# Memory's keys and values from split operands, and a later change of PSUM pools, in a Conformer and RWKV-7 streaming block

## The chip, the cores and the metric

The kernel runs on one core of one Trainium2 chip. The metric is the device time of one execution in microseconds (us), as the median of three runs. The engines are TensorE (PE, with its weight loads as PEld), VectorE (DVE), ScalarE (ACT), GpSimd (POOL) and SyncE (SP, which issues nearly all DMAs). [...]

## The reference, cut to what matters

One layer of a streaming encoder: x is 1024 frames by 1024 features, the memory 256 tokens by 1024.

```python
h = rmsnorm(x, g_mix)
p = h @ w_in                                  # 1024 conv columns, 1696 RWKV columns
u = p[:, :512] * sigmoid(p[:, 512:1024])      # conv branch
u = depthwise_causal_conv(u, conv_w, 31 taps) + conv_b
y_conv = silu(layernorm(u) * ln_g + ln_b)
y_rwkv = rwkv7(p[:, 1024:])                   # a recurrence over 1024 steps, 8 heads of 64
x = x + concat(y_conv, y_rwkv) @ w_out
k, v = rmsnorm(mem) @ wk, rmsnorm(mem) @ wv   # 4 heads of 256
x = x + softmax_attention(rmsnorm(x) @ wq, k, v) @ wo
x = x + relu(rmsnorm(x) @ w_ff1) ** 2 @ w_ff2
return rmsnorm(x, g_final)
```

## The kernel before

The kernel is one long program of a tile framework. The source emits instructions with a priority, which by default counts up in the order of the source. A planner then puts every engine's instructions in one fixed order: it plays the program through, and whenever an engine is free it hands it the ready instruction of the lowest priority number. On the chip each engine runs its list in that order and waits by semaphores only for real data. `at` and `shifted` (L421, L411) emit a piece under another priority. `fill` (L789) emits "side" steps 200 earlier than where they stand, and `tap` (L611) emits one step of the convolution 1000 earlier.

A float32 product is done in two ways. Most go through `mm3` (L75): both operands are split beforehand into a high part, rounded to the format `float32r` by ACT, and the rest, by a subtraction, and three products (high by high, high by low, low by high) add up in PSUM. A few take float32 as it is.

The stages and the buffers that order them:

- `mixer_in` (L525) computes `w_in`'s products for the first 512 frames and the convolution's for all. `tap_steps` (L615) is the convolution: five pieces (one channel block of 128 in two halves, three whole), each one multiplication (L646) and 30 multiply-adds on DVE (L649), of which 29 have PSUM (`sum`, two banks) as accumulator. At its end `mixer_in` calls `tap(1)` 31 times.
- Then the first PSUM pool `ps0` (banks `mm` 2, `pr` 2, `ep` 1, `cp` 1, `sum` 2) is closed and the second one, `ps` (`mm` 2, `pr` 2, `ep`, `cp`, `py`, `us` 1 each), is opened.
- The recurrence goes over eight tiles of 128 frames. `front(e)` (L772) is a tile's preparation (`rwkv_prepare`, L801: norms at L825 to L838, the products L871) and the triangular solve on DVE (`rwkv_solve`, L888: transposes L896, sixteen pairs L916 and L917, L921, L928, products L932 and L937, and the copy L938, which ends it). `chain(e)` (L778) is the recurrence proper, two chunks of 64 frames. Tile buffers `AR` and `BK` are two deep, so `front(e + 2)` waits for `chain(e)`.
- The order written out by hand: front 0, front 1, chain 0, front 2, chain 1, front 3, chain 2, and so on. Between them `fill` takes steps of a side generator, by the table `F`. The first side generator, `second_half` (L601), has twelve steps: each is one product of `w_in` for the second 512 frames, 24 matmuls of 128x512 (L81 to L83), with its weight split by ACT (L266) and POOL (L267), and a mixing step on ACT and DVE (L516, L517). `F` gives four of these steps to front 0, three to front 1 and the other five to chain 0.
- The second side generator (`side`, L341, from front 4 on in the source) interleaves `memory_side` (L449) with `conv_norms` (L712), then does `w_out` (`mix_steps`, L1051). `memory_side` takes float32 as it is: 8 + 8 weight blocks (`wkv`) of 128 columns against the normed memory (L461), and for each head the value times `wo` (L491, L494), which goes to DRAM as `dv`. `conv_norms` does the layer norm of the convolution for the eight tiles, on the buffers `x1`.
- Attention, the MLP (a seven-product scheme) and the last norm follow.

Of the kernel before, what the change touches and what calls it, by code (L numbers as in the profile page):

```python
# [17 lines left out]
P = 128  # L18
S = 1024
D = 1024  # L20
# [31 lines left out]
class Trunk:  # L52
# [220 lines left out]
    def run(self):  # L273
# [13 lines left out]
        with ctx:  # L287
# [32 lines left out]
            first.__exit__(None, None, None)  # L320
            self.ps = ctx.enter_context(self.pool("ps", space=PSUM, reuse_waits="tile"))
# [16 lines left out]
            x1 = {i: px1.tile([P, D], F32, name=f"x1_{i}") for i in (0, 4, 1, 5, 2, 6, 3, 7)}  # L338
            at = []

            def side():  # L341
                pn = push(right, "pN")
                norms = self.conv_norms(pn, x1)
                self.skip(pn, 288)
                pw, w = push(right, "pW0"), [None, None]
                for k, _ in enumerate(self.memory_side(push(right, "pM"), pw, w)):
                    if k % 2:
                        next(norms, None)
                    yield
                for _ in norms:  # L350
# [98 lines left out]
    def memory_side(self, pM, pw, wo):  # L449
        nc, a, ps = self.nc, self.a, self.ps  # L450

        mem = self.memT

        def m4(shape, name):
            return pM.tile(shape, F32, tag="m4", name=name, bufs=5)

        def half(name, c, dst):
            w = m4([P, KC, P], "wkv")
            nc.sync.dma_start(w, self.cols(name, c * P, P))
            for k in range(KC):  # L460
                nc.tensor.matmul(dst, w[:, k, :], mem[k // 4][:, k % 4, :], start=k == 0, stop=k == KC - 1)  # L461

        def features(name, g, out):
            pp = self.bank(ps, "mm")
            half(name, 2 * g, pp[:, 0:M])
            yield
            half(name, 2 * g + 1, pp[:, M:])
            nc.scalar.copy(out, pp.rearrange("p (e m) -> p e m", m=M))
            yield

        for g in range(4):
            t = pM.tile([P, 2, M], F32, tag="kv", name="kT", bufs=2)
            yield from features("wk", g, t)
            nc.sync.dma_start(self.dk[2 * g : 2 * g + 2].rearrange("e p m -> p e m"), t)
        for h in range(4):
            vT = pM.tile([P, 2, M], F32, tag="kv", name="vT", bufs=2)
            yield from features("wv", h, vT)
            if h == 2:
                wo[0] = self.out_weights(pw, lambda: m4([P, D], "wst")[:, 0:512], 0, 0)
            w = []  # L480
            for i in range(2):
                t = m4([P, D], "wo")
                nc.sync.dma_start(t, a["wo"][0, (2 * h + i) * P : (2 * h + i + 1) * P, :])
                w.append(t)
            for m in range(2):
                vs = m4([P, D], "vs")
                for n in range(2):
                    pp = self.bank(ps, "mm")
                    cs = slice(n * 512, n * 512 + 512)
                    for i in range(2):  # L490
# [34 lines left out]
    def mixer_in(self, pc, pb, px, pl, pW, pz, hT):  # L525
# [72 lines left out]
        for _ in range(31):  # L598
            self.tap(1)
# [999 lines left out]
```

## Time and profile before

| what | value |
|---|---|
| three runs | 1552.95, 1553.52, 1554.87 us; median 1553.52 |
| the profiled execution | 1554.8 us |
| its span, first to last instruction | 1553.1 us |
| mean granted TensorE clock | 0.982 |
| TensorE matmul | busy 1482.1 us (95%) |
| VectorE, ScalarE, GpSimd | busy 1119.4, 674.0, 519.4 us |

The profiled execution took 1554.8 us, of which 1.7 us lie outside its span. Matmuls are pipelined: the duration of a record is longer than the time until the next can start, so the number of matmuls in a stretch says more of PE's load than its busy time. A matmul on plain float32 leaves two records.

### The profile page before, as it was taken

The page shows a single profiled execution, that of the slowest core. Times are in us where ns is not written, and L with a number is a line of the kernel's source. Part 1 is how long each engine was busy: PE and PEld are TensorE (multiplying, and loading weights), DVE is VectorE, ACT ScalarE, POOL GpSimd, SP SyncE. Part 2 cuts the span into 40 slices and gives each one's busy share as a digit, 9 for nine tenths or more (in the row PEclk, how much of TensorE's full clock was granted, in tenths as well). Part 3 has the DMA queues.
Part 4 walks back from the last instruction along what each step waited for, and adds up shares of the span by engine and source line. Part 5 has one row for each costly group of instructions (what it writes and reads, how often), then busy time and mean ns, then how long its engine had stood idle before and what let it go on. Part 6 is the DMA issues. An engine that isn't in the chain of part 4 may idle for free. (4 is left out here: it accounts for less than half of the span.)

```text
span 1553.1 us, 22049 instructions
## 1 busy us (share of the span) xinstructions
PE 1482.1 (95%) x8114; PEld 1211.6 (78%) x8114; DVE 1119.4 (72%) x1701; ACT 674.0 (43%) x1243; POOL 519.4 (33%) x436
## 2 busy tenths in 40 slices
PE   5999995999999999999999979999999899999998
PEld 4777883778777778878888858888888788888886
DVE  5989995778788897464543797666666488587995
ACT  5433332423465543344222345555555445444454
POOL 4112453423335342331110064544444330003372
PEclk9999997999999999999999979999999999999999
DMA  7155563464234422221110223544444496552323
GB/s 211 55 169 173 153 175 102 134 190 123 62 116 143 143 96 76 88 89 48 35 42 27 81 96 116 172 157 153 150 153 152 170 366 204 184 183 87 103 81 122
DMA packets 175725, 201.14 MB, mean 130 GB/s; under 512 B 12191, under 2 KB 116951, under 8 KB 175618
## 3 DMA queue, kind: packets, MB, share of 16 engines
q1 hardware_dynamic: 168706, 187.15, 38.4%
q10 hardware_dynamic: 6912, 12.59, 2.2%
q8 instruction: 64, 1.05, 0.3%
q14 instruction: 43, 0.35, 0.1%
HBM read 139.92 MB, written 59.77 MB: 129 GB/s over the span
## 5 line engine op out<-in xcount | busy, mean ns | idle before, releaser
L649 DVE SCALAR_TENSOR_TENSOR sum<-u,cw,sum 128x1024 f32<-128x1024 f32 (+1 forms) x145 | 155.7, 1074 | 4.1
L1261 POOL TENSOR_TENSOR p<-p,p 128x512 f32<-128x512 f32 x32 | 61.0, 1935 | 196.6 <-DVE p L1520 171.8
L267 POOL TENSOR_TENSOR wlo<-wst,whi 128x1024 fp32r<-128x1024 f32 (+2 forms) x34 | 80.9, 2383 | 126.9 <-ACT whi L266 99.8
L73 DVE TENSOR_TENSOR s<-f,s 128x512 fp32r<-128x512 f32 x48 | 50.9, 1063 | 53.1 <-ACT s L72 53.1
L1366 ACT ACTIVATE y<-y 128x512 f32<-128x512 f32 x64 | 40.4, 632 | 80.8 <-DVE y L1261 73.3
L266 ACT CAST whi<-wst 128x1024 fp32r<-128x1024 f32 (+2 forms) x34 | 35.0, 1030 | 84.9 <-PE mm L82 25.9
L81 PE MATMUL mm<-hT1hi,whi 128*128 128x512 f32 (+1 forms) x128 | 51.5, 402 | 19.8 <-DVE z L517 19.8
L916 DVE TENSOR_TENSOR fs<-xt,PL 128x4 f32<-128x4 f32 (+15 forms) x128 | 61.8, 483 | 8.1 <-ACT PL L908 5.4
L461 PE MATMUL mm<-memT,wkv 128*128 128x256 f32 x256 | 63.4, 397 | 2.2 <-DMA wkv<-in_wk_dram 2.2
L95 POOL TENSOR_TENSOR rsr<-rsv,mhalf 128x1 f32<-128x1 f32 x26 | 15.2, 585 | 145.2 <-DVE rsv L90 135.6
L1261 POOL TENSOR_TENSOR s<-y 128x512 f32<-128x512 f32 x32 | 41.2, 1308 | 59.8 <-ACT y L1367 56.4
L72 ACT CAST s<-y 128x512 fp32r<-128x512 f32 x57 | 35.2, 621 | 58.3 <-PE us L83 26.8
L73 DVE TENSOR_TENSOR s<-y,s 128x512 fp32r<-128x512 f32 x57 | 44.9, 789 | 21.5 <-ACT s L72 21.5
L72 ACT CAST r<-y 128x512 fp32r<-128x512 f32 x55 | 33.8, 620 | 53.4 <-PE cp L83 23.2
L461 PEld LDWEIGHTS mm<-memT,wkv 128*128 128x128 f32 x256 | 48.4, 197 | 10.1 <-DMA wkv<-in_wk_dram 2.5
L72 ACT CAST s<-w 128x512 fp32r<-128x512 f32 x69 | 42.5, 618 | 22.9 <-DMA w<-in_w_ff_dram 8.0
L73 DVE TENSOR_TENSOR r<-y,r 128x512 fp32r<-128x512 f32 x55 | 42.6, 779 | 13.1 <-ACT r L72 13.0
L83 PE MATMUL mm<-hT1hi,wlo 128*128 128x512 f32 (+1 forms) x128 | 51.4, 401 | 0.0
L82 PE MATMUL mm<-hT1lo,whi 128*128 128x512 f32 (+1 forms) x128 | 50.9, 398 | 0.0
L72 ACT CAST s<-f 128x512 fp32r<-128x512 f32 x64 | 37.9, 620 | 27.6 <-DVE f L1261 22.1
L1104 POOL TENSOR_TENSOR wql<-wst,wqh 128x1024 fp32r<-128x1024 f32 x8 | 20.4, 2546 | 82.9 <-ACT wqh L1103 82.9
L917 DVE TENSOR_REDUCE xt<-fs 128x2 f32<-128x4 f32 (+15 forms) x128 | 45.2, 353 | 3.2
(1102 smaller groups left out, 4921.1 us busy)
## 6 DMA issues: line engine op xcount, KB each, us to landing
y<-da SPq DMA_DIRECT2D x112, 256.0 KB
wst<-in_w_in_dram SPq DMA_DIRECT2D x32, 512.0 KB
w<-in_w_ff_dram SPq DMA_DIRECT2D x56, 256.0 KB
da<-y ACTq DMA_DIRECT2D x48, 256.0 KB
ms<-in_w_ff_dram SPq DMA_DIRECT2D x16, 512.0 KB
w<-in_w_ff_dram SPq DMA_DIRECT2D x16, 512.0 KB
da<-s SPq DMA_DIRECT2D x32, 256.0 KB
da<-y SPq DMA_DIRECT2D x32, 256.0 KB
```

The lines of the kernel that those rows point to most:

```text
L72: nc.scalar.copy(hi, src)
L73: (eng or nc.vector).tensor_tensor(lo, src, f32(hi), ALU.subtract)
L81: nc.tensor.matmul(ps, lh, rh, start=first and k == 0, stop=False)
L82: nc.tensor.matmul(ps, lh, rl, start=False, stop=False)
L83: nc.tensor.matmul(ps, ll, rh, start=False, stop=last and k == n - 1)
L267: nc.gpsimd.tensor_tensor(lo, st, f32(hi), ALU.subtract)
L461: nc.tensor.matmul(dst, w[:, k, :], mem[k // 4][:, k % 4, :], start=k == 0, stop=k == KC - 1)
L649: nc.vector.scalar_tensor_tensor(acc if t < TAPS - 1 else out, u[:, t : t + w], self.cw[:, t * 4 + c : t * 4 + c + 1], acc, ALU.mult, ALU.add,
L916: nc.vector.tensor_tensor(tmp, x, rows, ALU.mult)
L917: nc.vector.tensor_reduce(xt[:, 0:m, 2 * k : 2 * k + 2], tmp, AX.X, ALU.add)
L1261: (eng or self.nc.vector).tensor_tensor(out, x, y, op)
L1366: nc.scalar.activation(c, c, AF.Relu)
```

## The change

The change has two parts. First, the pool `ps0` stays open over front 0 and front 1: the 31 calls of `tap` at the end of `mixer_in` go, the taps not yet emitted come with the side steps of these two fronts, and `ps` is opened ahead of chain 0. Second, `memory_side` splits the memory, its weights and the values and uses `mm3`; its weights' parts live in four tiles of its own and in the four `x1` buffers of tiles 4 to 7. So the convolution's norms get only four steps within it, and the other twelve after it; the split of `w_out`'s first block moves from the third head to the end.

```diff
@@ run
-            first.__exit__(None, None, None)
-            self.ps = ctx.enter_context(self.pool("ps", space=PSUM, reuse_waits="tile"))
             self.ring = None
...
             self.front(0)
             self.front(1)
+            for _ in self.taps:
+                pass
+            first.__exit__(None, None, None)
+            self.ps = ctx.enter_context(self.pool("ps", space=PSUM, reuse_waits="tile"))
             for e in range(3):
...
-            for _ in self.taps:
-                pass
             pop(right, 4)
...
-                for k, _ in enumerate(self.memory_side(push(right, "pM"), pw, w)):
-                    if k % 2:
-                        next(norms, None)
+                for k, _ in enumerate(self.memory_side(push(right, "pM"), pw, w, [(px1, f"x1_{i}") for i in range(4, 8)])):
+                    if 26 <= k < 30:
+                        next(norms)
                     yield
+                for i in range(4, 8):
+                    x1[i] = px1.tile([P, D], F32, tag=f"x1_{i}", name=f"x1_{i}")
                 for _ in norms:
                     yield
@@ memory_side
+        rooms = itertools.cycle([(pM, f"w{i}") for i in range(4)] + list(spare))
...
+        def parts(src, view):
+            st, hi, lo = stage(), room(), room()
+            nc.sync.dma_start(view(st), src)
+            nc.scalar.copy(hi, st)
+            nc.gpsimd.tensor_tensor(lo, st, f32(hi), ALU.subtract)
+            return view(hi), view(lo)
...
-                nc.tensor.matmul(dst, w[:, k, :], mem[k // 4][:, k % 4, :], start=k == 0, stop=k == KC - 1)
+                self.mm3(pp[:, e * M : (e + 1) * M], [(wh[:, k, :], wl[:, k, :]) for k in range(KC)], mem)
...
+            vh, vl = (pw.tile([P, 2, M], F32R, tag=t, name="vT") for t in ("wh3", "wl3"))
+            self.split(vh, vl, pp)
+            w = [parts(a["wo"][0, (2 * h + i) * P : (2 * h + i + 1) * P, :], lambda z: z) for i in range(2)]
...
-                    for i in range(2):
-                        nc.tensor.matmul(
-                            pp, vT[:, i, m * P : (m + 1) * P], w[i][:, cs], start=i == 0, stop=i == 1
-                        )
-                    nc.scalar.copy(vs[:, cs], pp)
+                    self.mm3(pp, [(vh[:, i, ms], vl[:, i, ms]) for i in range(2)], [tuple(z[:, cs] for z in w[i]) for i in range(2)])
+                    vs = pw.tile([P, HALF], F32, tag=("wh2", "wl2")[n], name="vs")
+                    nc.scalar.copy(vs, pp)
+                    nc.sync.dma_start(self.dv[h, m][:, cs], vs)
                     yield
-                nc.sync.dma_start(self.dv[h, m], vs)
+        wo[0] = self.out_weights(pw, lambda: stage(HALF), 0, 0)
@@ mixer_in
-        for _ in range(31):
-            self.tap(1)
```

The memory itself is split once: two ACT copies of 128x1024 to a room, four DVE subtractions of 128x512, and two more ACT copies of 128x1024 of the high part.

## Rows read from the trace of the kernel before

**Rows 1.** The page, busy time: engine, us (share) xinstructions

```profile
PE 1482.1 (95%) x8114; PEld 1211.6 (78%) x8114; DVE 1119.4 (72%) x1701; ACT 674.0 (43%) x1243; POOL 519.4 (33%) x436
```

**Rows 2.** By stretch: length, busy (x) of PE PEld DVE ACT POOL, PEclk, DMA, GB/s

```profile
232.50:252.20 19.70, 0.00 (x0) 0.00 (x0) 19.21 (x17) 3.85 (x6) 4.65 (x2) 0.56 0.10 31
252.20:318.00 65.80, 65.72 (x317) 50.67 (x317) 38.29 (x60) 21.83 (x37) 32.11 (x22) 0.97 0.47 135
...
339.80:552.20 212.40, 206.94 (x1777) 165.12 (x1779) 174.95 (x365) 108.31 (x211) 81.69 (x99) 0.98 0.42 124
552.20:659.00 106.80, 106.00 (x876) 88.23 (x877) 74.24 (x133) 39.00 (x79) 38.26 (x34) 1.00 0.27 86
...
1000.00:1200.00 200.00, 200.00 (x884) 165.65 (x883) 124.54 (x158) 104.08 (x171) 95.14 (x75) 1.00 0.46 153
```

**Rows 3.** Timeline of DVE, 211 to 253 us: start, us, instruction xcount [idle before]

```profile
211.87 0.74 DVE L517 SCALAR_TENSOR_TENSOR z<-mm,pcol,z 128x511 f32<-128x511 f32 x1
212.53 3.93 DVE L649 SCALAR_TENSOR_TENSOR sum<-u,cw,sum 128x1024 f32<-128x1024 f32 x3
...
229.09 21.16 DVE L649 SCALAR_TENSOR_TENSOR sum<-u,cw,sum 128x1024 f32<-128x1024 f32 x16
...
251.48 1.40 DVE L517 SCALAR_TENSOR_TENSOR z<-mm,pcol,z 128x511 f32<-128x511 f32 x2
```

**Rows 4.** Timeline of PE, 220 to 253 us

```profile
220.68 0.39 PE L81 MATMUL mm<-hT1hi,whi 128*128 128x512 f32 x1
...
231.65 0.82 PE L825 MATMUL pr<-s,bones_k 128*8 128x128 f32 x6
252.28 0.79 PE L81 MATMUL mm<-hT1hi,whi 128*128 128x512 f32 x1 [19.81 <-DVE z L517]
```

**Rows 5.** Timeline of ACT, 236 to 239 us

```profile
236.55 0.41 ACT L910 COPY xt<-start 128x256 f32<-128x256 f32 x1 [8.18 <-DMA start<-dl]
...
237.81 0.68 ACT L516 ACTIVATE z<-mm,omm 128x512 f32<-128x512 f32 x1
```

**Rows 6.** Timeline of SP, 325 us

```profile
325.89 2.15 SPq L717 DMA_DIRECT2D x<-dc  x4
```

**Rows 7.** Line 938, the end of a tile's solve: ns min/median/max, first and last start

```profile
L938 ACT COPY Z<-ep x8: 558/575/575, 327.0 to 623.5; 32x512 f32<-32x512 f32 x8
```

**Rows 8.** Timeline of PE: runs of one kind of product

```profile
386.79 2.54 PE L461 MATMUL mm<-memT,wkv 128*128 128x256 f32 x11
...
431.02 3.60 PE L491 MATMUL mm<-wo,vT 128*128 128x512 f32 x8
...
725.75 0.28 PE L83 MATMUL py<-kh,ql 128*128 128x256 f32 x1
...
726.83 0.28 PE L82 MATMUL us<-kl,qh 128*128 128x256 f32 x1
```

**Rows 9.** The staging tile wst: ACT's copies and POOL's subtractions, ns min/median/max

```profile
L266 ACT CAST whi<-wst x34: 612/1052/1055, 13.0 to 308.3; 128x1024 fp32r<-128x1024 f32 x32, 128x512 fp32r<-128x512 f32 x1, 128x768 fp32r<-128x768 f32 x1
L267 POOL TENSOR_TENSOR wlo<-wst,whi x34: 1678/2396/3101, 14.1 to 312.1; 128x1024 fp32r<-128x1024 f32 x32, 128x512 fp32r<-128x512 f32 x1, 128x768 fp32r<-128x768 f32 x1
```

**Rows 10.** Timeline of PE, 325 to 337 us: one tile's small products

```profile
325.79 1.19 PE L937 MATMUL ep<-Z,V 32*32 32x32 f32 x32
326.91 1.71 PE L871 MATMUL pr<-AR,BK 64*128 64x128 f32 x16
```

**Rows 11.** Timeline of DVE, the solves of tiles 0 and 1

```profile
290.40 4.00 DVE L896 STREAM_TRANSPOSE PL<-T 32x1024 f32<-32x1024 f32 x2
...
298.38 2.32 DVE L916 TENSOR_TENSOR fs<-xt,PL 128x32 f32<-128x32 f32 x1
...
319.25 1.42 DVE L928 STREAM_TRANSPOSE Z<-XD 32x512 f32<-32x512 f32 x2
...
346.49 0.19 DVE L916 TENSOR_TENSOR fs<-xt,PL 128x32 f32<-128x32 f32 x1
```

**Rows 12.** One stretch, instructions that touch whi: PE (x), PEld (x), ACT (x), POOL (x)

```profile
252.20:318.00 65.80, 47.96 (x146) 27.47 (x146) 8.38 (x8) 19.43 (x8) 0.97 0.47 135
```

More of the change, by code (lines that the diff above doesn't have):

```diff
@@ L333, in run @@
             self.finish()
[L334 to L335 removed]
             pop(right, 4)
             px1 = push(right, "px1")
[L338 removed]
+            x1 = {}
+            for i in (0, 4, 1, 5, 2, 6, 3, 7):
+                x1[i] = px1.tile([P, D], F32, tag=f"x1_{i}", name=f"x1_{i}")
             at = []
@@ L445, in memory_in, with memory_side @@
             nc.scalar.activation(self.memT[k // 4][:, k % 4, :], pp[:, :M], AF.Identity, scale=self.col("g_mem", k))
-    def memory_side(self, pM, pw, wo):
+    def memory_side(self, pM, pw, wo, spare):
         nc, a, ps = self.nc, self.a, self.ps
[L452 to L460, printed above, removed]
-                nc.tensor.matmul(dst, w[:, k, :], mem[k // 4][:, k % 4, :], start=k == 0, stop=k == KC - 1)
-        def features(name, g, out):
-            pp = self.bank(ps, "mm")
-            half(name, 2 * g, pp[:, 0:M])
-            yield
-            half(name, 2 * g + 1, pp[:, M:])
-            nc.scalar.copy(out, pp.rearrange("p (e m) -> p e m", m=M))
-            yield
[L471 to L480, printed above, removed]
-            for i in range(2):
-                t = m4([P, D], "wo")
-                nc.sync.dma_start(t, a["wo"][0, (2 * h + i) * P : (2 * h + i + 1) * P, :])
-                w.append(t)
@@ new lines, in memory_side, with room, stage @@
+        rooms = itertools.cycle([(pM, f"w{i}") for i in range(4)] + list(spare))
+        def room():
+            pool, tag = next(rooms)
+            return pool.tile([P, D], F32R, tag=tag, name="wkv")
+        def stage(n=D):
+            return pM.tile([P, n], F32, tag="st", name="wst", bufs=2)
+        def parts(src, view):
[4 more added lines that the diff above has]
+            return view(hi), view(lo)
@@ new lines, in memory_side @@
+        high, low = [], []
+        for i, t in enumerate(self.memT):
+            hi = room()
+            nc.scalar.copy(hi, t.rearrange("p k m -> p (k m)"))
+            for j, tag in enumerate((f"wh{i}", f"wl{i}")):
+                lo = pw.tile([P, 2, M], F32R, tag=tag, name="memL")
+                two = slice(2 * j, 2 * j + 2)
+                nc.vector.tensor_tensor(
+                    lo, t[:, two], f32(hi).rearrange("p (k m) -> p k m", m=M)[:, two], ALU.subtract
+                )
+                low += [lo[:, k, :] for k in range(2)]
+            t = self.pm.tile([P, 4, M], F32R, tag="ms", name="memH", bufs=2)
+            nc.scalar.copy(t, f32(hi).rearrange("p (k m) -> p k m", m=M))
+            high += [t[:, k, :] for k in range(4)]
@@ new lines, in memory_side, with features @@
+        mem = list(zip(high, low))
+        def features(name, g):
+            pp = self.bank(ps, "mm")
+            for e in range(2):
+                wh, wl = parts(self.cols(name, (2 * g + e) * P, P), lambda z: z.rearrange("p (k f) -> p k f", f=P))
+                self.mm3(pp[:, e * M : (e + 1) * M], [(wh[:, k, :], wl[:, k, :]) for k in range(KC)], mem)
+                if e == 0:
+                    yield
+            return pp.rearrange("p (e m) -> p e m", m=M)
+        for g in range(4):
+            pp = yield from features("wk", g)
+            t = pw.tile([P, 2, M], F32, tag=("wh2", "wl2")[g % 2], name="kT")
+            nc.scalar.copy(t, pp)
+            nc.sync.dma_start(self.dk[2 * g : 2 * g + 2].rearrange("e p m -> p e m"), t)
+            yield
@@ L485, in memory_side @@
+        for h in range(4):
+            pp = yield from features("wv", h)
+            vh, vl = (pw.tile([P, 2, M], F32R, tag=t, name="vT") for t in ("wh3", "wl3"))
+            self.split(vh, vl, pp)
+            w = [parts(a["wo"][0, (2 * h + i) * P : (2 * h + i + 1) * P, :], lambda z: z) for i in range(2)]
+            yield
             for m in range(2):
-                vs = m4([P, D], "vs")
+                ms = slice(m * P, (m + 1) * P)
                 for n in range(2):
```

2 lines of the change are left out of this document (1 added, 1 removed).

## The prediction, made blind

> **What bounds the kernel now.** I read the page first, then busy times by stretch, then the timelines of single engines around the place where a pool changes hands. PE is busy 95% of the span, far ahead of DVE, so the question for each edit is whether PE gets shorter or is fed better [rows 1]. By stretch, one thing stands out: from 232.5 to 252.2 us PE runs nothing at all, for 19.7 us, while DVE is busy 19.2 of them [rows 2]. What ends that hole is one mixing step on DVE, L517, which frees a bank of PSUM; DVE got to it only after 16 taps in one block and a last one [rows 3, 4]. Twenty us earlier the same mixing step slipped in between taps as soon as its product was done [rows 3]. So taps don't always go first.
>
> Why did it not slip in here? The orders of the engines tell. The first product of the second 512 frames ran on the chip at 220.68, in the middle of the taps, so the chip needed no wait for them; but its mixing step on ACT stands behind a copy that came at 236.55, and tile 0's first norm products (L825) stand behind two whole side products, though nothing else was there for PE [rows 4, 5]. All of these write or read the new pool `ps`; what stands ahead of them on ACT and DVE needs no bank of it. I read this as a rule of the planner: it hands out no bank of a new pool until the whole old pool is free, here until the last tap. Other pools show the same: the loads of the convolution's result by the next pool's tiles come together at 325.9, some 70 us after the last tap, when the side products are done [rows 3, 6].
>
> Later, from 340 to 659 us, PE is visibly idle for only 212.4 - 206.9 + 106.8 - 106.0 = 6.3 us, with DVE at 175 of 212 beside it: PE's own work and the recurrence's loop run side by side [rows 2]. The recurrence ends a solve every (623.5 - 327.0) / 7 = 42.4 us [rows 7].
>
> **The change, part by part.** Prices first. Matmul records overlap, so a pitch is taken from runs. Plain float32 of 256 columns: (2.54 - 0.38) / 10 = 0.216 us per record, two records each, 0.432. Of 512 columns: (3.60 - 0.59) / 7 = 0.430, two records, 0.860. Split operands: 200 / 884 = 0.227 for 512 columns, and for 256 nine steps from 725.75 to 726.83, 0.120 [rows 2, 8]. (0.38 and 0.59 are the durations of one record in these runs.)
>
> *Memory's products.* Keys and values are 16 blocks of 8 steps: 128 x 0.432 = 55.3 us become 384 x 0.120 = 46.1. The products with `wo` are 32 x 0.860 = 27.5 us and become 96 x 0.227 = 21.8. PE is relieved of 9.2 + 5.7 = 14.9 us. [...]
>
> *Its feeding.* 24 blocks more are split: 24 ACT copies at 1.05 and 24 POOL subtractions at 2.4 us, that is 25 and 58 us, and some 4 us of ACT and 6 of DVE for the memory and the values [rows 9]. In the 212 us in which this runs, ACT has 108 and POOL 82 us to do, so both have room [rows 2]; SP issues eight more stores and the same loads, and `dv` is read only in the attention, long after. The first block now needs 3.5 us between landing and product. I charge +1 us; between 0, if all hides, and +15, if the whole relief is lost (the last rival).
>
> *The taps.* Counting the calls: 150 steps are taken before the 31 calls, 155 exist. So 26 of the 31 calls are empty, and five taps move. They keep their priority: 1000 ahead, now 1200 ahead of a place about 100 further on. What matters is the pool. The first side products and tiles 0 and 1 stay in `ps0`, nothing of theirs waits for the last tap, the mixing steps slip in between taps as they did before, and the 19.7 us close.
>
> *What is late next.* By the same rule no bank of `ps` is given until `ps0` is free, and now front 1 is in `ps0`: the pool opens when tile 1's solve ends (L938). Until then PE has seven of the twelve side products, 7 x 24 x 0.227 = 38 us, and two tiles' small products, some 9.5 us each (two runs of 1.71 for L871, 1.19 each for L932 and L937, the rest about 3.5 by the same size) [rows 10]. From 220.5 these last until 278. When does tile 1's solve end? Tile 0's ended at 327.6, about 75 us after the hole's end at 252.3, behind which its last norm product stood [rows 4, 7]. Begun at the next gap between side products, at 226 to 232, it would end at 301 to 307; I take 296, as PE is nearly empty after 278 and no POOL subtraction meets the solve. Tile 0's solve took 30.3 us from its first to its last transpose (290.4 to 320.7), with at least one step stretched by 2 us, and 7 more to the end of L938 [rows 7, 11]. Tile 1's can begin when tile 0's last transposes leave the buffer, some 4 us before 296, and without side work I take 26 us for it: **318**. Had it to run beside chain 0, as in the kernel before, where the loop's pace is 42 us a tile, it would be about 338.
>
> By 318 the kernel before had done 2 + 146 x 1.5 / 24 = 11.1 side products (two thirds of a product's matmuls touch `whi`) [rows 12]. After, it has done seven: 4.1 x 5.45 = 22 us of PE's work are pushed past 318. In return tile 1's 9.5 us are done there already, and about 2 us of chain 0 are not. Net **+15 us** of backlog at 318. The 19.7 us that close are inside this account.
>
> *The lead.* At 318 tiles 0 and 1 are both solved, where before tile 0 ended at 327.6 and tile 1 one loop step, some 42 us, later, at about 370. Chain 1 then follows chain 0 (some 30 us) at about 348 instead of 370 or later, and at the loop's pace all of the recurrence is 20 to 30 us earlier [rows 7]. PE then has less to wait for: between 0 and the 6.3 us it visibly waits. I take -6, as the lead is several times that. The norms behind the memory cost PE nothing more; at most they leave `w_out`'s products without input for a while, and the recurrence covers that.
>
> Sum: +15 - 14.9 + 1 - 6 = -5 us on 1554.8, which is 1549.8 as profiled; the profiled execution is 1.3 us above the median of the three runs, so **1548.5**. A measurement of this kernel can tell about 0.2%, 3.1 us, from no change.
>
> **The rivals.**
>
> *No hole (faster).* If the pool rule holds only for the banks that are really in use, `ps` opens with the last tap and the gap closes without a new one: 19.7 us, 2 us of low clock after it (PEclk 0.97 over 65.8 us), and 14.9 go: 1517. For it speaks that the chip itself ran the new pool's product at 220.68; against it, the three lists above.
>
> *The gap stays (the change does not do what it says).* The five taps keep their priority and 26 calls were empty, so if priority alone made DVE's block, the order stays as it is: 1554.8 - 14.9 + 1, 1540 against the median. Against it: mixing steps passed taps of the same priority at 211.87 [rows 3].
>
> *The pool opens late (slower).* Same place, `ps` behind L938 of tile 1. Each us after 318 is a us in which PE has nothing it may start; the sum turns at 323 and is slower by 0.2% from 326. If tile 1's solve keeps its old distance from tile 0's, it ends near 338: 1568. For it: prices of front 1 without chain 0 are nowhere in the trace.
>
> *POOL holds the solves (slower).* In tile 0's solve L916 took 2.32 us where the same step took 0.19 in tile 1's: a 2.4 us subtraction of a weight was running beside it [rows 9, 11]. [...] 24 such subtractions more, each stretching a solve by up to 2 us where it meets one, are up to 48 us in the memory's stretch, where DVE has 37 us left of 212. If half meet a solve, 25 us, the lead is mostly gone and PE waits more: +5 to +15 on the forecast, 1560.
>
> **How the numbers follow.** The forecast has 0.42, split by where 318 really lies: 0.25 faster, 0.12 the same, 0.05 slower; its own range is 1538 to 1558. No hole 0.13, the gap stays 0.12: both faster. The pool opens late 0.20: 0.17 slower, 0.03 the same. POOL holds the solves 0.13: 0.10 slower, 0.03 the same. Together 0.50 faster, 0.18 the same, 0.32 slower. The range goes from the faster rival to the late pool: 1518 to 1570 (338 and two more us for the estimates in it).
>
> **What would show it.** In the profile after: no wait of PE for L517 near 232; L517 between taps to the end; then, right if a stretch with few matmuls lies between about 270 and 318, with chain 0 and the last five side products behind tile 1's L938. Wrong if the last side products run ahead of it. Memory's groups at L81 to L83 with 0.120 us pitch, and their products starting near 360, not 340. L916's mean above 0.43 us in the memory's stretch would speak for POOL. The last L938 should lie near 590, not 623.5.

## The result, and the profile after

The changed kernel takes 1619.64 us (1618.57 to 1625.24) against 1554.12 of the kernel before: a ratio of 1.043, 95% interval 1.0404 to 1.0455. That is 65.5 us slower, where 5 us faster was forecast, and outside the range. The execution in the profile took 1625.24 us, with a span of 1623.5 and a mean granted clock of 0.948. Lines from L449 on stand lower down in the changed file; in the recurrence L916 became L936, L938 became L958, and a tap is L669.

The page's busy line of the changed kernel answers to [rows 1]:

```profile
PE 1509.3 (93%) x8274; PEld 1254.7 (77%) x8274; DVE 1154.7 (71%) x1709; ACT 692.3 (43%) x1263; POOL 578.1 (36%) x460
```

TensorE is busy 27 us longer than before, although its work has become 15 us shorter by the prediction's own prices. POOL has 59 us more, as forecast for 24 subtractions of 2.4 us. VectorE has 35 us more, though it got only 8 instructions more, which take under 8 us together. So two engines spend longer on the same work, and that is the first thing to explain.

By stretch, the changed kernel (columns as in [rows 2]):

```profile
232.50:252.20 19.70, 19.70 (x91) 15.71 (x90) 18.81 (x18) 8.55 (x14) 13.42 (x8) 1.00 0.62 173
...
263.70:326.60 62.90, 25.93 (x211) 22.59 (x210) 49.68 (x99) 9.85 (x19) 11.16 (x14) 0.52 0.13 36
326.60:334.00 7.40, 7.40 (x27) 5.96 (x25) 0.00 (x0) 0.58 (x1) 0.00 (x0) 0.73 0.00 0
375.80:618.20 242.40, 219.65 (x1966) 194.65 (x1967) 206.51 (x336) 107.71 (x200) 141.48 (x119) 0.87 0.35 110
618.20:764.40 146.20, 135.12 (x894) 110.98 (x893) 92.56 (x164) 67.06 (x135) 48.53 (x46) 0.93 0.24 77
```

The old gap of 19.7 us is filled: TensorE is busy for all of 232.5 to 252.2. In its place stands a stretch of 62.9 us, from 263.7 to 326.6, in which TensorE works 25.93 us at a granted clock of 0.52. The memory's products run from 375.8 to 618.2, 242.4 us, where the kernel before needed 211.8 (339.8 to 551.6); they start 36 us late and end 67 us late. From their end to the last product of `w_out` it takes 146.2 instead of 135.2 us.

TensorE's timeline at the end of the new hole (start, us, instruction, and in brackets the idle time before it with what ended it):

```profile
290.39 2.07 PE L902 MATMUL pr<-s,bones_r 128*128 128x128 f32 x8
304.10 1.91 PE L952 MATMUL ep<-XD,T 32*32 32x32 f32 x32 [11.63 <-DVE XD L941]
...
322.23 1.88 PE L952 MATMUL ep<-XD,T 32*32 32x32 f32 x32 [13.51 <-DVE XD L941]
324.82 1.91 PE L957 MATMUL ep<-Z,V 32*32 32x32 f32 x32 [0.71 <-ACT V L954]
326.66 0.80 PE L81 MATMUL mm<-hT1hi,whi 128*128 128x512 f32 x1
327.25 0.63 PE L82 MATMUL mm<-hT1lo,whi 128*128 128x512 f32 x1
327.68 0.63 PE L83 MATMUL mm<-hT1hi,wlo 128*128 128x512 f32 x1
```

The last solve's product ends at 326.7, and at 326.66 the next side product begins: 0.43 us after one another at first, where the granted clock is 0.50 (326.6 to 328.0 us), against 0.227 at a clock of 1.00 [rows 2]. That the second pool had held it is shown by `e8_twopools` in section 5. Of the seven side products done in fronts 0 and 1 the last ended at 262.

All eight solves, by the copy that ends each (ns min/median/max, first and last start):

```profile
L958 ACT COPY Z<-ep x8: 559/576/578, 308.8 to 662.7; 32x512 f32<-32x512 f32 x8
```

The first comes 18 us earlier than in [rows 7], the last 39 us later. The lead that the change gives to the first two tiles is lost, and more, within the memory's stretch.

### The profile page after: what moved, and what is told of

Its sections match the earlier page's. It is cut to its first block, busy times and chain, and to the rows that moved or that the text cites. A ratio compares the mean times of both kernels' runs of the same rounds, so it can differ in the third digit from the quotient of the medians.

```text
span 1623.5 us, 22492 instructions
## 1 busy us (share of the span) xinstructions
PE 1509.3 (93%) x8274; PEld 1254.7 (77%) x8274; DVE 1154.7 (71%) x1709; ACT 692.3 (43%) x1263; POOL 578.1 (36%) x460
## 5 line engine op out<-in xcount | busy, mean ns | idle before, releaser
L669 DVE SCALAR_TENSOR_TENSOR sum<-u,cw,sum 128x1024 f32<-128x1024 f32 (+1 forms) x145 | 155.7, 1073 | 3.9
L936 DVE TENSOR_TENSOR fs<-xt,PL 128x4 f32<-128x4 f32 (+15 forms) x128 | 73.9, 578 | 12.6 <-ACT PL L928 9.6
L468 POOL TENSOR_TENSOR wkv<-wst,wkv 128x1024 fp32r<-128x1024 f32 x24 | 60.6, 2528 | 12.0 <-ACT wkv L467 10.3
L891 PE MATMUL pr<-AR,BK 64*128 64x128 f32 x256 | 40.9, 341 | 16.9 <-DVE BK L881 8.7
L891 PEld LDWEIGHTS pr<-AR,BK 64*128 64x128 f32 x256 | 35.6, 237 | 20.2 <-POOL wkv L468 7.5
```

What stands on the lines that cost most here:

```text
L468: nc.gpsimd.tensor_tensor(lo, st, f32(hi), ALU.subtract)
L669: nc.vector.scalar_tensor_tensor(acc if t < TAPS - 1 else out, u[:, t : t + w], self.cw[:, t * 4 + c : t * 4 + c + 1], acc, ALU.mult, ALU.add,
L891: nc.tensor.matmul(pp[:, p, :], BK[rows, 2 * p + c, :], AR[rows, 2 * p + c, :], start=True, stop=True)
L936: nc.vector.tensor_tensor(tmp, x, rows, ALU.mult)
```

## The experiments

Every difference below is against the runs of the kernel before on the same chip.

### 1. The two parts of the change, each alone

`e1_pools` has the changed pools and taps, with the memory's side of the kernel before. `e2_memory` is the reverse. Their diffs are the two halves of the change.

> Only the pool part is taken over: ps opens after front 1 and the remaining taps come with the side steps; the memory's side is that of the kernel before, float32 as it is, with its norms interleaved. Theory A (two separate losses: the hole before the second pool, then the split memory): in the changed kernel the first memory product started 36 us late (375.8 against 339.8), and the kernel before has under 10 us of idle TensorE after that in which to win it back, so about 1554 + 36 = 1590, between 1580 and 1595. Theory B (all of the loss is POOL's subtractions in the memory's stretch, the hole is won back by the lead of tile 1): 1563 or less, as the pool part by itself was forecast at +15 - 6. Theory C (the low clock after the hole does it, and it returns only where the gaps return): 36 us late at the memory's start too, but no gaps afterwards, 1590 as A.

> Only the memory part is taken over: split operands, the norms behind them; pools and taps are those of the kernel before. Theory A (the split memory is a loss of its own): the memory's stretch lasted 242.4 us instead of 211.8 and the stretch from its end to the end of w_out's products 146.2 instead of 135.2, so 1554 + 31 + 11 = 1596, at least 1580. Theory B (the memory lost only because it came late and met chains 0 to 2 with TensorE at its low clock): the relief of 15 us holds, 1540. Theory D (half of it each): about 1570.

`e1_pools`: 1582.91 us, ratio 1.0197 (1.0179 to 1.0215), +29.2 us. `e2_memory`: 1606.43 us, ratio 1.0341 (1.0326 to 1.0357), +52.7 us. Each part is a loss by itself, as theory A had it, and neither B nor C nor D holds. Together they would be 82 us, where both at once cost 66; a part of the two losses seems to be the same lateness, which no run here separates.

For `e1_pools` the trace tells the loss apart. By stretch, from 340 to 720 us in both kernels, first the kernel before:

```profile
340.00:720.00 380.00, 371.32 (x2951) 302.23 (x2952) 288.65 (x559) 176.91 (x346) 137.60 (x147) 0.99 0.34 104
```

And `e1_pools`, with the memory's products and what follows them in rows of their own:

```profile
340.00:720.00 380.00, 367.01 (x2923) 297.73 (x2922) 268.06 (x506) 173.52 (x341) 138.63 (x149) 0.99 0.38 114
376.80:578.70 201.90, 196.41 (x1694) 157.67 (x1694) 163.20 (x329) 103.15 (x204) 80.45 (x97) 0.99 0.42 129
578.70:707.10 128.40, 128.40 (x934) 106.59 (x933) 84.81 (x148) 47.05 (x94) 39.38 (x35) 1.00 0.26 81
```

The memory's first product comes 37 us late (376.8 against 339.8). Its stretch is then 10 us shorter (201.9 against 211.8) and the one behind it 7 us (128.4 against 135.2), which is the work of tile 1 already done and some of the lead. The norms that follow let TensorE wait 5 us longer (716.0 - 707.1 against 690.7 - 686.8). 37 - 10 - 7 + 5 = 25, and the span is 1578.7 - 1553.1 = 25.6 us longer. So the hole is paid with 37 us, of which 17 come back. From 340 to 720 us the clock is 0.99, as before: theory C falls.

For `e2_memory` the expectation had the right size and the wrong place. Its memory's products took 212 us, no longer than before (341 to 554), but the last solve ended at 660 instead of 624, and the last product of `w_out` came at 737 instead of 687. The loss is one of the recurrence, not of the memory.

### 2. POOL's subtractions: left out, unread, on VectorE

```diff
 # e3_nolow
-            st, hi, lo = stage(), room(), room()
+            st, hi = stage(), room()
+            next(rooms)
...
-            nc.gpsimd.tensor_tensor(lo, st, f32(hi), ALU.subtract)
-            return view(hi), view(lo)
+            return view(hi), view(hi)
 # e5_unread: the subtraction stays
-            return view(hi), view(lo)
+            return view(hi), view(hi)
 # e6_on_dve
-            nc.gpsimd.tensor_tensor(lo, st, f32(hi), ALU.subtract)
+            nc.vector.tensor_tensor(lo, st, f32(hi), ALU.subtract)
```

> The changed kernel without POOL's 24 subtractions: the high part stands in for the low part of the weights (the output's memory branch is then another number; left out are the low parts of wk, wv and wo). TensorE, ACT and the DMAs do the same work. Theory A1 (POOL's subtractions stretch VectorE's instructions with two SBUF operands, L936 at 0.65 us against 0.44, and with them every solve): L936 falls to about 0.45 us, the memory's stretch to 215 us or less, and the time by 25 to 40 us, to 1580 to 1595. Theory A2 (the stretch is long because the norms no longer fill TensorE and the blocks arrive late through ACT): L936 falls too, but the time by less than 10 us, 1610 or more.

> The changed kernel with POOL's 24 subtractions in their places, but TensorE multiplies the high part in place of the low one, so that nobody waits for what POOL writes (left out are the low parts of wk, wv and wo, as in e3_nolow). It differs from e3_nolow (1580.6) by POOL's work alone and from the changed kernel (1619.6) by the wait for it alone. Theory A1 (POOL's work itself stretches VectorE and stands in POOL's queue ahead of the recurrence): the mean of L936 stays above 0.6 us and the time at 1605 to 1620. Rival (TensorE waits for the low parts): the time falls to 1580 to 1590, with the mean of L936 still above 0.6.

> The changed kernel with its 24 subtractions of weights on VectorE instead of POOL. Theory A1 (a subtraction on POOL costs VectorE its own 2.4 us, where it meets instructions with two SBUF operands, so VectorE might as well do it in about 1.2 us): L936 falls to about 0.46 us, VectorE has 24 x 1.2 = 29 us more to do, and the time falls to 1595 to 1612, above e3_nolow by 15 to 30. Rival (VectorE's own load bounds the recurrence, so 29 us more of it cost as much as POOL does): 1619 or more.

`e3_nolow`: 1580.61 us, +26.9, so 39 us of the 66 go with the subtractions. `e5_unread`: 1616.10 us, +61.7. POOL does all of them and no product reads what it writes; 35 of the 39 us are back. The wait of TensorE for the low parts is worth at most the other 4, which the intervals don't tell from nothing. One wait is left in this run: the next block's load still waits until POOL has read the staging tile (13 times, 34.5 us from 340 to 720 us). In the changed kernel, which has it too, the trace shows none of it at TensorE: of the 34.6 us in the same stretch in which TensorE waits, 24 end with VectorE and none with a block of the memory's weights; in `e3_nolow` 5 of 15 us end with VectorE. `e6_on_dve`: 1603.77 us, +49.4: VectorE is better off doing them itself, by 16 us, although that loads it with 24 instructions of 1.225 us (median).

The groups of the solve's step in the recurrence's stretch (320 to 700 us; busy us, mean ns | idle before, releaser), for the kernel before, the changed kernel, `e3_nolow`, `e5_unread` and `e6_on_dve` in turn:

```profile
L916 DVE TENSOR_TENSOR fs<-xt,PL 128x4 f32<-128x4 f32 (+7 forms) x112 | 49.4, 441 | 6.9 <-ACT PL L908 4.6
```

```profile
L936 DVE TENSOR_TENSOR fs<-xt,PL 128x512 f32<-128x512 f32 (+7 forms) x97 | 63.0, 650 | 7.1 <-ACT PL L928 4.9
```

```profile
L936 DVE TENSOR_TENSOR fs<-xt,PL 128x4 f32<-128x4 f32 (+7 forms) x96 | 44.8, 466 | 3.8 <-ACT PL L928 1.7
```

```profile
L936 DVE TENSOR_TENSOR fs<-xt,PL 128x4 f32<-128x4 f32 (+7 forms) x96 | 63.4, 661 | 11.1 <-ACT PL L928 8.9
```

```profile
L936 DVE TENSOR_TENSOR fs<-xt,PL 128x512 f32<-128x512 f32 (+7 forms) x97 | 46.7, 481 | 9.2 <-ACT PL L928 7.4
```

With POOL at work the mean is 0.65 to 0.66 us, without it 0.47 to 0.48; the kernel before has 0.44. One place in the changed kernel shows it. First VectorE alone, where POOL does nothing (281 and 295 us), then all engines at 460 to 470:

```profile
281.42 0.69 DVE L881 TENSOR_TENSOR BK<-a,sig 128x512 f32<-128x512 f32 x1
...
295.10 0.57 DVE L936 TENSOR_TENSOR fs<-xt,PL 128x392 f32<-128x392 f32 x1
```

```profile
459.71 2.67 POOL L468 TENSOR_TENSOR wkv<-wst,wkv 128x1024 fp32r<-128x1024 f32 x1 [0.94 <-ACT wkv L467]
460.75 2.06 DVE L936 TENSOR_TENSOR fs<-xt,PL 128x392 f32<-128x392 f32 x1
...
467.03 2.62 POOL L468 TENSOR_TENSOR wkv<-wst,wkv 128x1024 fp32r<-128x1024 f32 x1
467.37 2.83 DVE L881 TENSOR_TENSOR BK<-a,sig 128x512 f32<-128x512 f32 x1
...
470.34 0.98 PE L891 MATMUL pr<-AR,BK 64*128 64x128 f32 x3 [7.36 <-DVE BK L881]
```

The same instruction on the same shapes takes 2.06 us instead of 0.57, and 2.83 instead of 0.69, each ending 0.4 to 0.6 us after POOL's subtraction (462.38 and 469.65): about its own length, as if it had begun only then. TensorE needs `BK` next, and starts as it is there, after a wait of 7.4 us. By the durations alone the two stretches make `BK` up to 1.5 + 2.1 us later; VectorE's other steps fill the rest. (For the same wait the weight load's record names POOL's subtraction, which had ended 0.7 us before.) Over the 24 subtractions, the VectorE instructions that ran beside one took 39 us longer than the shortest of the same form in the kernel before; 19 of the 24 made one longer by more than 0.3 us. Nearly all of it lies with forms that read two operands from SBUF: 20 us with L936, 4 each with L881 and `kp`; the transposes that ran beside one lost 0.2 us together.

The reading that fits these rows is that the instruction on VectorE waits for the end of the subtraction, and that the two don't run side by side at a lower pace; by what means, no run shows.

What follows this gap costs as well. TensorE in the changed kernel, by stretch, around that wait:

```profile
462.98:470.30 7.32, 0.00 (x0) 0.00 (x0) 7.25 (x9) 1.50 (x2) 5.17 (x4) 0.78 0.33 109
470.30:485.00 14.70, 14.66 (x102) 12.78 (x103) 8.79 (x15) 4.05 (x8) 4.42 (x7) 0.50 0.22 73
```

After 7.3 us without a matmul TensorE is busy 14.66 of 14.7 us at a granted clock of 0.50. From 340 to 720 us the changed kernel stands like this:

```profile
340.00:720.00 380.00, 345.35 (x2877) 296.65 (x2877) 281.81 (x470) 172.94 (x330) 190.97 (x163) 0.89 0.34 107
```

It is idle 34.7 us and runs the rest at 0.89, which is worth another 0.11 x 345 = 38 us. `e1_pools` has 13.0 us idle and 0.01 x 367 = 3.7 us in the same stretch. By this estimate 56 us of TensorE are lost; less the relief of 15 us it makes 41. The changed kernel is 1619.64 - 1582.91 = 36.7 us slower than `e1_pools` by the medians, and 1623.5 - 1578.7 = 44.8 by the two spans.

### 3. Where the relief of 15 us went

`e3_nolow` has no subtraction left and still is only 2.3 us faster than `e1_pools`, where the shorter products should give 14.9. Two runs ask why: `e7_norms` puts the norms back into their old places, and `e11_two_products` makes TensorE's work shorter still.

```diff
 # e7_norms, on top of e3_nolow
-        rooms = itertools.cycle([(pM, f"w{i}") for i in range(4)] + list(spare))
+        rooms = itertools.cycle([(pM, f"w{i}") for i in range(4)])
...
-                    if 26 <= k < 30:
-                        next(norms)
+                    if k % 2:
+                        next(norms, None)
...
 # e11_two_products, on top of e7_norms, in the memory's calls of mm3
             nc.tensor.matmul(ps, lh, rl, start=False, stop=two and last and k == n - 1)
+            if two:
+                continue
             nc.tensor.matmul(ps, ll, rh, start=False, stop=last and k == n - 1)
```

> e3_nolow with the norms of the convolution interleaved with the memory's steps as in the kernel before (the weights' high parts take four tiles, the x1 tiles are not used for them; left out are the low parts, as there). In e3_nolow the last product of w_out ended 76 us after the recurrence's last L958, in the kernel with the pool part alone 65 us, in the kernel before 63. Theory N (norms behind the memory make w_out's products late): these 11 to 13 us come back, 1566 to 1572, which is the kernel with the pool part alone less the relief of 15 us (1582.9 - 14.9 = 1568). Rival (the place of the norms costs nothing, the relief is lost elsewhere): 1577 to 1584.

> e7_norms with the third of the three products left out (the weights' low part times the memory's high part; in e7 both parts were the high one, so the memory's branch is again another number): TensorE has 128 x 0.120 + 32 x 0.227 = 22.6 us less to do in the memory's stretch, with everything else in its place. Theory S (what the split relieves on TensorE turns into waits for the recurrence and a lower granted clock): the time stays within 6 us of e7_norms, 1572 to 1580, and the clock of the memory's stretch falls further below 0.95. Rival (TensorE's work bounds the stretch, and the relief of 15 us was lost to something that the split adds): 1553 to 1562.

`e7_norms`: 1577.82 us, +23.4 (ratio 1.0145, 1.0129 to 1.0162). Theory N falls: of 11 to 13 us, 3.5 came back, about as much as the intervals leave open. `e11_two_products`: 1579.04 us, +24.6 (1.015, 1.013 to 1.0171): 22.6 us less of products gained nothing, as theory S had it. The same stretch as above for `e7_norms` and then for `e11_two_products`:

```profile
340.00:720.00 380.00, 367.33 (x3078) 316.37 (x3077) 274.69 (x512) 199.12 (x367) 138.54 (x149) 0.95 0.36 111
```

```profile
340.00:720.00 380.00, 353.50 (x2934) 298.48 (x2933) 274.16 (x513) 199.12 (x366) 142.98 (x149) 0.94 0.38 115
```

`e7_norms` is idle as long as `e1_pools` (12.7 us against 13.0) with a clock of 0.95 against 0.99: 0.04 x 367 = 15 us, as much as the relief (where the idle time lies differs, as the last section shows), and the two spans are equal (1578.4 and 1578.7 us). By the medians some 6 of the 15 us came through (29.2 - 23.4). ACT's 24 copies of blocks, which the split adds, cost 7 us by themselves in `e13_act_copy` below, so a part of the relief may have gone there; how it divides is not shown. `e11_two_products` gives its further 22.6 us back as 14 us more of idle time and 0.01 more of low clock. In this stretch a shorter product on TensorE is not a shorter stretch, although its 206.9 of 212.4 busy us [rows 2] had looked like a bound. That it is the recurrence's loop that sets the pace is the reading that fits, from who ends the waits (the steps of solve and chain); the runs show only that TensorE's length does not.

### 4. POOL's, ACT's and nobody's work added to the kernel before

Is it POOL's work, or only another order of instructions? These kernels are the kernel before with one or more instructions for each of the 24 blocks of weights and nothing else:

```diff
             nc.sync.dma_start(w, self.cols(name, c * P, P))
+            nc.gpsimd.tensor_tensor(t, t, t, ALU.add)            # e9_pool_alone
+            nc.gpsimd.tensor_copy(t, t)                          # e10_one_input
+            nc.gpsimd.tensor_copy(t[:, 0:8], t[:, 0:8])          # e12_tiny; e15_three_tiny: three of them
+            nc.scalar.copy(t, t)                                 # e13_act_copy
+            nc.gpsimd.tensor_tensor(t[:, 0:1], self.mask[:, 0:1], self.mask[:, 0:1], ALU.pow)   # e16_pow_column
```

(`t` is the block as 128x1024, for `wk` and `wv` after the load shown, for `wo` after its own.)

> The kernel before with nothing but 24 instructions of POOL more: each of the 24 blocks of wk, wv and wo is added to itself in place, 128x1024 float32 with two SBUF operands, as long as a subtraction (so these weights are doubled; pools, taps, products and norms are those of the kernel before). Theory A1 (POOL's work on SBUF stretches VectorE's instructions with two SBUF operands, and so every solve): L916's mean after 340 us rises from 0.44 to 0.6 us or more, the recurrence's last L938 moves from 624 to 650 or later, and the time to 1580 to 1595. Rival (POOL only hurts where the split memory is there, with its late norms and short products): 1554 to 1565.

> As e9_pool_alone, but POOL copies each block onto itself: one SBUF operand instead of two. If any of POOL's work on SBUF holds VectorE for its own length, the cost per us of POOL is as in e9_pool_alone, and the time lies above 1554 by that share. If only POOL's two operands do it, L916's mean stays below 0.48 us and the time within 5 us of 1554.

> As e10_one_input, but POOL copies only 8 of each block's 1024 columns: 24 instructions in the same places, with next to no work and no stretch of anything. Theory W (what costs is the time that POOL, or a block on its way through POOL, takes): within 4 us of 1554. Rival O (24 instructions more let the planner put the engines' instructions in another order, and the order of the kernel before happens to be a good one): 1565 to 1582, near e10_one_input's 1581.6, although POOL has nothing to do.

> As e10_one_input, but ACT copies each block onto itself, in about 1.05 us, instead of POOL: what the split memory adds on ACT, by itself. Theory W (the block's way through one more engine costs, whichever it is): about e10_one_input's 1581.6, or 12 to 27 us above 1554; then the relief of 15 us that e7_norms and e3_nolow did not show was paid here. Rival (ACT has room, 108 us busy of 212): within 5 us of 1554.

> As e12_tiny, with three such copies of 8 columns per block instead of one. POOL's work is again next to nothing, but now the planner puts the engines' instructions in another order than in the kernel before (in e12_tiny the order of all other instructions stayed the same, so that run said nothing of the order). Rival O (another order alone costs what e10_one_input cost): 1565 to 1582. Theory W (the time on POOL costs): within 6 us of 1555.

> As e12_tiny, with a power on POOL into the first column of each block in place of the copy (that column of the weights is then 1): one column, but about 0.58 us of POOL by the kernel's other powers of one column, 14 us in all, and again another order. Rival O: 1565 to 1582. Theory W: by e10_one_input's price (27 us for 25.7 us of POOL) at most 15 us, 1555 to 1570; if it is SBUF traffic that costs and not POOL's time, within 6 us of 1555.

| kernel | added, us of engine time | time, us | ratio, 95% | L916's mean, us |
|---|---|---|---|---|
| e12_tiny | POOL, 4.6 (24 of 0.19); same order | 1555.82 | 1.0002 (0.9986 to 1.0018) | 0.43 |
| e15_three_tiny | POOL, 13.8 (72 of 0.19); other order | 1554.52 | 1.0000 (0.9986 to 1.0014) | 0.45 |
| e16_pow_column | POOL, 13.2 (24 of 0.55); other order | 1560.74 | 1.0044 (1.0028 to 1.0060) | 0.46 |
| e13_act_copy | ACT, 25.1 (24 of 1.05); other order | 1562.35 | 1.0049 (1.0027 to 1.0071) | 0.45 |
| e10_one_input | POOL, 25.7 (24 of 1.07); other order | 1581.58 | 1.0174 (1.0144 to 1.0204) | 0.49 |
| e9_pool_alone | POOL, 47.1 (24 of 1.96); other order | 1584.30 | 1.0190 (1.0175 to 1.0206) | 0.58 |

Another order, even with 13.8 us of POOL's time in short pieces, cost nothing (`e15_three_tiny`), so rival O falls as a general price; that one particular order is a bad one is not excluded by it. `e12_tiny` could not tell this, as the order of all other instructions stayed what it was, and its copies, forecast as next to nothing, took 0.19 us each. `e9_pool_alone` came as theory A1 had it: the last solve moved from 624 to 652 us, and the mean, 0.58, stayed a little under the 0.6 that was expected. `e16_pow_column`, at +7 us, lies in the range of theory W, but also within 6 us of 1555, so it does not tell POOL's time from SBUF traffic. `e13_act_copy` lies between its two expectations: ACT's copies cost 7 us, a quarter of what POOL's do.

`e10_one_input` fits neither of its theories. The groups of POOL's copies and VectorE's solve step in it:

```profile
L458 POOL COPY wkv<-wkv 128x1024 f32<-128x1024 f32 x16 | 17.2, 1083 | 17.0 <-DMA wkv<-in_wk_dram 9.1 <-PE mm L465 6.1 <-DMA wkv<-in_wv_dram 1.1
...
L458 POOL COPY wo<-wo 128x1024 f32<-128x1024 f32 x8 | 8.5, 1077 | 2.8 <-DMA wo<-in_wo_dram 2.8
```

```profile
L921 DVE TENSOR_TENSOR fs<-xt,PL 128x4 f32<-128x4 f32 (+7 forms) x112 | 54.8, 489 | 4.3 <-ACT PL L913 1.9
```

VectorE's instructions beside these copies took 10 us longer (26 in `e9_pool_alone`), yet the time rose by 27. From 340 to 760 us TensorE is idle 23 us instead of 9, and up to 720 us it runs at 0.94 instead of 0.99. So two fifths of the stretch cost nearly the whole price, and the longer steps of VectorE are not the only way in which POOL's work costs. A block that is later is hardly the other: of TensorE's 24 us of waits up to 720 us, one of 2.0 us ends with a copy. Whether the rest comes through the recurrence's own steps behind a copy in POOL's queue, a bad order of the planner's, or the lower granted clock (0.94 against 0.99), these runs don't tell apart; it is left open.

### 5. The hole: filled, or never opened

`e4_sides` gives fronts 0 and 1 all twelve side products. `e8_twopools` takes the other way: the memory and its norms are those of the kernel before, the taps those of the changed kernel, and only the two banks that really change hands are in a pool that closes (the tiles `sum`, `py` and `us` are taken from `ps2`, all others from `ps`). `e14_two_sides` has both.

```diff
 # e4_sides; e14_two_sides: the same on top of e8_twopools
-F = ((2, 2, 3), (2, 1, 3),
+F = ((2, 4, 3), (3, 3, 3),
 # e8_twopools
             first = self.pool("ps0", space=PSUM, reuse_waits="tile")
-            self.ps = first.__enter__()
+            self.ps = ctx.enter_context(self.pool("ps", space=PSUM, reuse_waits="tile"))
+            self.ps2 = first.__enter__()          # sum alone
...
             first.__exit__(None, None, None)
-            self.ps = ctx.enter_context(self.pool("ps", space=PSUM, reuse_waits="tile"))
+            self.ps2 = ctx.enter_context(self.pool("ps2", space=PSUM, reuse_waits="tile"))   # py and us
```

> The changed kernel with all twelve side products given to fronts 0 and 1 (four more in the first, five in the second become 6 and 6), none to chain 0. Theory A (the hole from 263 to 326 us is lost because five side products stand behind the second pool): they fill it, TensorE keeps its clock, the memory starts 25 to 36 us earlier and the time falls to 1583 to 1595. Rival (their splits on POOL and mixing steps on DVE hold tile 1's solve, and the pool opens that much later): the solve ends at 345 instead of 327 and the time stays within 10 us of 1619.

> The kernel before's memory, with the taps as in the changed kernel, but the banks mm, pr, ep and cp stay in one pool from start to end, and only the two banks of sum are a pool that is closed after the taps and opened again as py and us; so of all that follows only chain 0 stands behind the taps and front 1. Theory G (the planner gives no bank of a new pool until the whole old one is free, in the kernel before at the last tap, after the change at tile 1's L958): neither the gap of 19.7 us nor the hole from 263 to 326 appears, TensorE keeps its clock, and the time is 1530 to 1540. Rival (DVE's taps or the recurrence's loop bound that stretch anyway): the gap closes and comes back as waits of chain 0, 1548 to 1556.

> e8_twopools (1539.3) with all twelve side products in fronts 0 and 1, as in e4_sides. With two pools there is no hole for them to fill, TensorE is busy throughout from 220 to 340 us either way, so what changes is only which work comes first: chain 0 loses its fillers. Expected within 6 us of e8_twopools if TensorE's work bounds that stretch, 1545 to 1560 if the recurrence's start is what counts and the side products' splits and mixing steps hold it.

`e4_sides`: 1591.59 us, +37.8, so 28 us less than the changed kernel, as theory A had it. The rival was partly right as well: tile 1's solve ended at 343 instead of 327, since the splits of five more weights ran beside it. The memory began at 348.3 instead of 375.8.

`e8_twopools`: 1539.34 us, ratio 0.9906 (0.9882 to 0.9930): 15 us faster than the kernel before and 80 faster than the changed one. By stretch:

```profile
232.50:252.20 19.70, 19.70 (x95) 16.10 (x94) 18.74 (x19) 8.97 (x16) 12.49 (x7) 1.00 0.60 167
252.20:318.00 65.80, 65.80 (x414) 53.28 (x413) 47.16 (x76) 21.85 (x40) 24.67 (x23) 0.92 0.52 150
340.00:720.00 380.00, 368.54 (x2876) 299.76 (x2877) 278.82 (x535) 175.88 (x349) 129.04 (x140) 0.98 0.31 97
```

Neither the gap nor the hole is there: TensorE is busy for all of 232.5 to 318 us, and the solves end sooner:

```profile
L939 ACT COPY Z<-ep x8: 574/574/579, 304.5 to 603.9; 32x512 f32<-32x512 f32 x8
```

The last solve ends at 603.9 against 623.5 in [rows 7], 20 us sooner, and the memory's first product comes at 321.8 instead of 339.8. From `e1_pools`, which has the same memory and the same taps, this kernel differs by the pools alone. So the rule of the planner that the prediction had only argued is shown for the hole: what held the work was not the two banks of `sum`, but that all eight banks were one pool. For the gap of the kernel before it is the reading that fits, since there the taps' place differs too. `e14_two_sides` takes 1540.68 us (0.9901, 0.9881 to 0.9921): with no hole to fill, the side products' place makes no difference that can be told.

## Why the prediction was wrong

It had the hole right and its price wrong, it lost the relief to something that it did not look at, and it charged the feeding 1 us where it costs 39. The three terms measured: +29 for the pools (forecast +15 - 6), -2 for the rest of the memory's part, the shorter products above all (forecast -14.9), +39 for POOL's work (forecast +1). Together 66 us, where -5 was forecast.

**The pool rule** held. The gap closed, the mixing steps slipped in between the taps (at 237.0, 242.2 and 248.0 us), and chain 0 with the last five side products stood behind tile 1's L958. The rivals "no hole" and "the gap stays" fell.

**When it opens.** The step "I take 296" for tile 0 and "**318**" for tile 1 was 13 and 9 us early: the copies that end the solves came at 308.8 and 326.8. The last norm product of tile 0 and the first transpose of its solve, in the kernel before (for the transpose see [rows 11], 290.40) and then in the changed one:

```profile
253.43 0.60 PE L825 MATMUL pr<-s,bones_k 128*8 128x128 f32 x2
```

```profile
226.78 1.04 PE L845 MATMUL pr<-s,bones_k 128*8 128x128 f32 x8
...
269.67 3.84 DVE L916 STREAM_TRANSPOSE PL<-T 32x1024 f32<-32x1024 f32 x2
```

The old distance of 75 us, counted from 226.8, would have ended the solve at 302; the prediction took 6 off that for an empty TensorE. The steps between these rows took 43 us instead of 37: they wait their turn behind side products on TensorE (L851 came at 244.15, 4.3 us after its input) and, after the change, behind taps on VectorE too (the last at 257.95). The solve took 40 us instead of 37. Tile 1 followed tile 0 by 18 us, where 22 were forecast. "The pool opens late" was the rival for this; it put the turn at 323 us and 326 at 0.2% slower. At 326.8 this gives 4 us by the prediction's own sum, not 29.

**What the hole costs.** The term "+15" left out two things. Behind the hole TensorE runs at a granted clock of 0.73 over the 7.4 us from 326.6 to 334.0, which is 2 us; and 9 us come from the late opening. 15 + 9 + 2 = 26. In `e1_pools` the memory began 37 us late, and tile 1's products, which the term takes off, came back as a stretch 10 us shorter: 27, within 1 us of that sum. "The lead", put at -6, came as -7 in the stretch behind the memory (tile 1 of the kernel before was solved at 381 us, not "at about 370", so the lead was longer than forecast and gave hardly more), and the norms' longer wait at the end, 5 us, took most of it again. That makes 25 by the trace and 29 by the medians.

**The relief.** "PE is relieved of 9.2 + 5.7 = 14.9 us" counted products in a stretch that TensorE's length does not set. Section 3 shows it: 22.6 us more of relief gained nothing, and of the 14.9 some 6 came through. The prediction had read that "PE's own work and the recurrence's loop run side by side" and then charged only one of the two.

**The feeding.** "So both have room", and with it "I charge +1 us", is the step that failed most. Room on POOL is not room on VectorE: 19 of the 24 subtractions held a step of VectorE, most often the solve's L936, and TensorE's waits that ended with VectorE are 24 us, against 5 without the subtractions. The rival "POOL holds the solves" named POOL's subtractions, the place and L916's mean above 0.43 us (it was 0.65), and was given 0.13 and +5 to +15 us. Its bound of 48 us stood in the text; "DVE has 37 us left of 212" was taken as slack, though the solve is a chain in which each stretched step is late at once. The measured stretch of 39 us lies near that bound. `e10_one_input` shows that the stretch is not the whole of what POOL's work costs; the rest stays open.

**The norms** cost little, as was said: `e7_norms` gains 3.5 us.

## What to carry to other kernels

Before moving work to an idle engine, ask which other engine's instructions wait for it while it runs: here a step on VectorE took 2 us longer beside 2.6 us on POOL (2.83 us against 0.69), and the same 24 subtractions on the busier VectorE were 16 us cheaper. With this planner a pool that changes hands holds all its banks for the last of them; put only the banks that really change into the pool that closes. Where two loops run side by side at 97% busy, shortening one of them may be worth nothing until the other is shown to be shorter.

## What the runs showed of the hardware

A copy on POOL with one SBUF operand, 1.08 us, cost as much of the time (27 us for 24) as an addition with two, 1.9 us (30 us), though it stretched VectorE's steps by 10 us instead of 26.

About the same idle time of TensorE went with different granted clocks from 340 to 720 us. With the memory's float32 products, 13.0 us of idle time went with 0.99 (`e1_pools`); with split products, 12.7 us went with 0.95 (`e7_norms`) and 14.9 with 0.94 (`e3_nolow`). The kind of product need not be the cause: 5.9 of the 13.0 us of `e1_pools` come after 700 us, behind the memory's stretch, so that up to 700 us it is idle 7.1 us and `e7_norms` 12.7; and `e10_one_input`, with float32 products and 23.2 us of idle time, stands at 0.94. Why is not shown.
